# Order of the expert groups in the dense stage of a hybrid decoder block: stored first products spread among the others

## The chip, the core and the metric

The kernel runs on one core of one Trainium2 chip. The metric is the device time of one execution in microseconds (us), lower is better. PE is TensorE, DVE is VectorE, ACT is ScalarE, POOL is GpSimd, and SP is the engine whose queue starts most of the DMA transfers. A number such as L1254 is a line of the kernel before.

## What is computed

The reference is one layer of a decoder for 1024 tokens of width 1024: two attention branches, a memory attention, and a mixer with 16,384 experts of which each token uses 128. The last part is the one in question:

```python
def chunk(args):
    hc, ic, gc = args
    a = jnp.einsum('cd,ced->ce', hc, u[ic])
    a = jax.nn.gelu(a, approximate=False) * gc.astype(hc.dtype)
    return jnp.einsum('ce,ced->cd', a, v[ic])
```

`ic` holds the 128 chosen experts of each token and `gc` their weights. The sum over the experts may be taken in any order.

## The kernel before

The tokens are handled in eight blocks of 128. For blocks 0 to 3 the chosen rows of `u` and `v` are gathered from DRAM, one row per token at a time. POOL starts each gather (L1035 for `u`, L1051 for `v`) into a ring of seven tiles `rows`, and DVE multiplies and sums the gathered tile (L1038 for `u`, L1057 for `v`). This is a side stream: a pacer (`Pace`) hands out one gather for every so many estimated microseconds of PE work, 2.0 in the dense stage (`U_EACH[-1]`).

For blocks 4 to 7, 512 tokens together, all experts are computed densely, in 128 tiles of 128 experts (`dense`, L1192). Per tile there is a first product (`first`, L1210: 24 matmuls with the tile `uT`, after `uraw` was loaded and split on ACT and DVE into two parts), a gelu, a multiplication with the expert weights `wl` (L1254, on DVE; a weight is zero where the token did not choose the expert), a split of the result into the two parts `c0` and `c1` (ACT L112, DVE L113), and a second product with the rows of `v` (L1278, after `vraw` was loaded and split, 24 matmuls per tile). Tiles go in groups of four: `group` (L1241) makes the four operands `c`, `second` (L1260) does 96 matmuls with them. The loop asks for `group` of the next group before `second` of the present one. Four of the eight accumulators stay in PSUM (`kept`); the other four (`out`) are added to SBUF by DVE after each group (`accu`, L1283).

The first 48 tiles (`EARLY`) have their first product done in an earlier stage, in which the weights are made. Their gelu is stored to DRAM (`ga`), and in the dense stage `group` only loads it back (L1250) instead of computing it. I call the twelve groups of these tiles early groups, and the other twenty full groups.

Three buffers matter. The reloaded gelu has one buffer (`c`, L1249), so the load for the next early tile starts only after the multiplication of the one before. `wl` has two buffers, each for two tiles (L1245), so a new one can be loaded only when both tiles of the pair before last are split. And the operands `c0`, `c1` have seven buffers (L1255) where two groups would need eight, so the last split of a group waits for the end of the second product before it.

All engines take their instructions in the order in which they were built. That order comes from the order of the code and from priorities that lag the gathers; nothing is reordered when it runs.

Of the kernel before, what the change touches and what calls it, by code (L numbers as in the profile page):

```python
# [84 lines left out]
class K:  # L85
# [1106 lines left out]
    def dense(self, psum, early):  # L1192

        nc, a = self.nc, self.a
        blks = list(range(NG, NB))
        V = a["peer_v"][0]
        NE = P
        with ExitStack() as ctx:
            E = ctx.enter_context
            up = E(self.pool("up"))  # L1200
            h3 = self.h3T

            def load_u(e):
                raw = up.tile([P, D], F32, name="uraw", bufs=U_BUFS)
                self.last_load = nc.sync.dma_start(raw, a["peer_ut"][e]).ins
                uT = [up.tile([P, KD, P], F32R, name=f"uT{j}", bufs=2) for j in range(2)]
                self.split(raw.rearrange("p (k c) -> p k c", k=KD), uT[0], uT[1])
                return uT

            def first(e):  # L1210
                uT = load_u(e)
                o = self.acc()
                for k in range(KD):
                    self.mm3(o, [u[:, k] for u in uT], [x[:, k] for x in h3], k == 0, k == KD - 1)
                self.pace.tick(KD * 3 * 0.216)
                return o

            ga = {}
            with ExitStack() as c2:
                self.wb = c2.enter_context(self.pool("wb"))  # L1220
                self.u_each = U_EACH[-2]
                self.pace.add("weights", self.weights(blks))
                for e in range(early):
                    o = first(e)
                    t = self.wb.tile([P, 512], F32, name="gelu", bufs=2)
                    nc.scalar.activation(t, o, AF.Gelu)
                    ga[e] = self.scratch([P, 512], f"ga{e}")
                    nc.sync.dma_start(ga[e], t)
                self.pace.drain("weights")
            self.route_ctx.close()  # L1230
            psum = self.psum_phase(psum, "ps3", A_BUFS)
            kept = {}
            for n in range(KEEP):
                i, d = n % ND, n // ND
                kept[i, d] = self.ps.tile([P, 512], F32, name=f"kept{n}", bufs=1)
            self.u_each = U_EACH[-1]
            sp = E(self.pool("sp"))
            accu = sp.tile([P, ND, D], F32, name="accu")
            G = 4

            def group(gi):  # L1241
                cs = []
                for e in range(gi * G, gi * G + G):
                    if e % 2 == 0:
                        w2 = sp.tile([P, 2 * ND, 2, P // 2], F32, name="wl", bufs=2)  # L1245
                        nc.sync.dma_start(w2, self.Wd[:, :, e:e + 2].rearrange("j p e n -> p j e n"))
                    w = w2[:, :, e % 2]
                    if e in ga:
                        c = sp.tile([P, DT], F32, name="c", bufs=1)  # L1249
                        nc.sync.dma_start(c, ga[e])  # L1250
                    else:
                        c = first(e)
                        nc.scalar.activation(c, c, AF.Gelu)
                    nc.vector.tensor_tensor(w, c.rearrange("p (j n) -> p j n", j=2 * ND), w, op=OP.mult)  # L1254
                    ch = [sp.tile([P, DT], F32R, name=f"c{j}", bufs=7) for j in range(2)]  # L1255
                    self.split(w, *[x.rearrange("p (j n) -> p j n", j=2 * ND) for x in ch])
                    cs.append(ch)
                return cs

            def second(gi, cs):  # L1260
                vs = []
                for e in range(gi * G, gi * G + G):
                    vv = [sp.tile([P, D], F32R, name=f"v{j}", bufs=V_BUFS[j]) for j in range(2)]
                    raw = sp.tile([P, D], F32, name="vraw", bufs=V_BUFS[2])
                    nc.sync.dma_start(raw, V[e * P:(e + 1) * P])
                    self.split(raw, vv[0], vv[1])
                    vs.append(vv)
                for i in range(ND):
                    for d in range(2):
                        ds = slice(d * 512, (d + 1) * 512)  # L1270
                        keep = (i, d) in kept
                        o = kept[i, d] if keep else self.ps.tile([P, 512], F32, name="out", bufs=O_BUFS)
                        last = gi == NE // G - 1
                        for j in range(G):
                            self.mm3(o, [c[:, i * P:(i + 1) * P] for c in cs[j]], [v[:, ds] for v in vs[j]],
                                     j == 0 and (gi == 0 or not keep), j == G - 1 and (last or not keep))
                        if keep:
                            if last:  # L1278
                                nc.scalar.activation(accu[:, i, ds], o, AF.Copy)
                        elif gi == 0:  # L1280
                            nc.scalar.activation(accu[:, i, ds], o, AF.Copy)
                        else:
                            nc.vector.tensor_tensor(accu[:, i, ds], accu[:, i, ds], o, op=OP.add)  # L1283
                        self.pace.tick(G * 3 * 0.216)

            cs = group(0)
            for gi in range(NE // G):
                nx = group(gi + 1) if gi + 1 < NE // G else None
                second(gi, cs)
                cs = nx  # L1290
            for i, b in enumerate(blks):
                t = [up.tile([P, D], F32, name="uraw", bufs=U_BUFS) for _ in range(2)]
                self.finish(b, accu[:, i], t if i else t + [sp.tile([P, D], F32, name="vraw", bufs=V_BUFS[2])])
        return psum
# [136 lines left out]
```

## Time and profile before

| | us |
|---|---|
| median of three runs | 3481.64 |
| lowest and highest run | 3471.62 and 3495.5 |
| the profiled execution | 3480.88 |
| span of its trace | 3479.1 |

The profiled execution is as long as the median run to within 0.02%. Its span starts with the first instruction; 1.8 us lie outside. The dense stage starts at about 2200 us; the early groups run to about 2540 and the full groups from there to the end. Waits in a trace are given as the idle time of an engine before an instruction and the event that ended it.

### The profile page before, as it was taken

To read this page: it belongs to the slowest core of one execution; us is meant where nothing else is said; L and a number is where in the kernel's file an instruction comes from. 1 tells how busy PE (TensorE), PEld (TensorE's weight loads), DVE (VectorE), ACT (ScalarE), POOL (GpSimd) and SP (SyncE) were. 2 spreads that over 40 slices of the span, in tenths; PEclk is the share of its full clock that TensorE was granted. 3 is DMA by queue.
4 is the path that set the end of the run, shared out by engine and by line. 5 is a ranking of instruction groups with operands and counts; after the bars stand their busy time and mean duration, and the time that the engine had idled before them with its cause. 6 is when DMAs were issued, how large, how long until landed. Compare 5 with 4: busy or idle time off the path is not lost. (4 is left out here: it accounts for less than half of the span.)

```text
span 3479.1 us, 42293 instructions
## 1 busy us (share of the span) xinstructions
PE 3023.2 (87%) x13234; PEld 2293.0 (66%) x13234; DVE 2849.2 (82%) x6623; ACT 1404.7 (40%) x2537; POOL 1396.1 (40%) x1122
## 2 busy tenths in 40 slices
PE   8999888798788798777899897588899999999997
PEld 6778765553345675545777675466677887877886
DVE  6656544588969889888999899677799999999998
ACT  5756344345656451322455557222122222222222
POOL 0010000011245346554123566334456666676664
PEclk9999998899888799778999999799899999999999
DMA  4575444435699479888567999999999999999997
GB/s 139 164 183 139 164 140 138 134 121 182 197 299 317 139 246 366 308 319 299 167 222 272 381 384 389 360 303 309 312 348 375 379 378 357 368 384 379 382 376 269
DMA packets 394209, 964.64 MB, mean 277 GB/s; under 512 B 36712, under 2 KB 146048, under 8 KB 392576
## 3 DMA queue, kind: packets, MB, share of 16 engines
q0 software_dynamic: 155264, 560.01, 45.4%
q1 hardware_dynamic: 238720, 401.94, 33.7%
q8 instruction: 104, 1.70, 0.2%
q14 instruction: 121, 0.99, 0.1%
HBM read 871.64 MB, written 90.18 MB: 276 GB/s over the span
## 5 line engine op out<-in xcount | busy, mean ns | idle before, releaser
L1035 POOL DMA_INDIRECT rows<-in_peer_u_dram,ii x512 | 679.8, 1328 | 903.9 <-DVE rows L1038 284.2
L1051 POOL DMA_INDIRECT rows<-in_peer_v_dram,ii x512 | 652.9, 1275 | 419.8 <-DVE h3s L1057 269.0
L1057 DVE SCALAR_TENSOR_TENSOR h3s<-rows,wexp,h3s 128x1024 f32<-128x1024 f32 x508 | 650.8, 1281 | 34.9 <-DMA rows<-in_peer_v_dram,ii 26.0
L1038 DVE SCALAR_TENSOR_TENSOR rows<-rows,h3s 128x1024 f32<-128x1024 f32 x512 | 610.2, 1218 | 72.5 <-DMA rows<-in_peer_u_dram,ii 72.1
L135 PE MATMUL acc<-fT,uT 128*128 128x512 f32 x1024 | 417.0, 407 | 39.1 <-ACT uT L112 21.7
L137 PE MATMUL acc<-fT,uT 128*128 128x512 f32 x1024 | 410.1, 400 | 3.1 <-DVE uT L113 3.0
L136 PE MATMUL acc<-fT,uT 128*128 128x512 f32 x1024 | 409.8, 400 | 0.0
L112 ACT ACTIVATE c<-wl 128x512 fp32r<-128x512 f32 x128 | 80.0, 631 | 758.9 <-PE out L136 458.9
L149 POOL TENSOR_TENSOR rstd<-msq,mhalf 128x1 f32<-128x1 f32 (+1 forms) x42 | 34.4, 819 | 595.1 <-DVE msq L147 578.3
L135 PEld LDWEIGHTS acc<-fT,uT 128*128 128x128 f32 x1024 | 195.9, 191 | 85.2 <-ACT uT L112 22.1
L136 PE MATMUL kept<-v,c 128*128 128x512 f32 x512 | 206.1, 406 | 38.0 <-DVE v L113 37.9
L135 PE MATMUL kept<-v,c 128*128 128x512 f32 x512 | 201.7, 400 | 38.1 <-ACT v L112 38.1
L137 PEld LDWEIGHTS acc<-fT,uT 128*128 128x128 f32 x1024 | 195.4, 191 | 59.3 <-issue 12.3
L112 ACT ACTIVATE uT<-uraw 128x1024 fp32r<-128x1024 f32 x128 | 135.6, 1059 | 235.8 <-PE acc L136 162.0
L136 PEld LDWEIGHTS acc<-fT,uT 128*128 128x128 f32 x1024 | 195.9, 191 | 39.6 <-issue 0.7
L135 PE MATMUL out<-v,c 128*128 128x512 f32 x512 | 203.9, 398 | 9.3 <-DVE accu L1283 9.3
L113 DVE TENSOR_TENSOR w<-wraw,w 128x512 fp32r<-128x512 f32 (+1 forms) x176 | 116.4, 679 | 116.2 <-ACT w L112 109.2
L137 PE MATMUL kept<-v,c 128*128 128x512 f32 x512 | 204.3, 399 | 0.0
L136 PE MATMUL out<-v,c 128*128 128x512 f32 x512 | 203.5, 397 | 0.0
L137 PE MATMUL out<-v,c 128*128 128x512 f32 x512 | 203.3, 397 | 0.0
L568 ACT ACTIVATE junk<-W,xb 128x384 bf16<-128x384 f32 (+5 forms) x186 | 163.7, 880 | 78.4 <-DVE xb L566 75.6
L133 PE MATMUL acc<-wraw,hT 128*128 128x512 f32 (+1 forms) x384 | 168.7, 593 | 15.7 <-ACT tok L355 10.0
(361 smaller groups left out, 6710.7 us busy)
## 6 DMA issues: line engine op xcount, KB each, us to landing
uraw<-in_peer_ut_dram SPq DMA_DIRECT2D x128, 512.0 KB, 8.6
vraw<-in_peer_v_dram SPq DMA_DIRECT2D x128, 512.0 KB, 8.7
Wd<-wbuf SPq DMA_DIRECT2D x64, 512.0 KB, 9.1
wl<-Wd SPq DMA_DIRECT2D x64, 512.0 KB, 9.6
wraw<-in_w_in_dram SPq DMA_DIRECT2D x40, 512.0 KB, 3.7
fraw<-in_w_in_dram SPq DMA_DIRECT2D x32, 512.0 KB, 5.8
wraw<-in_w_out_dram SPq DMA_DIRECT2D x24, 512.0 KB, 3.7
ga<-gelu SPq DMA_DIRECT2D x48, 256.0 KB, 5.3
```

Of the source, the lines that this page charges most:

```text
L112: self.nc.scalar.activation(hi, src, AF.Copy)
L113: self.last_dve = self.nc.vector.tensor_tensor(lo, src, hi.bitcast(F32), op=OP.subtract).ins
L133: self.last_pe = nc.tensor.matmul(out, l[0], r[0], start=start, stop=stop).ins
L135: nc.tensor.matmul(out, l[0], r[0], start=start, stop=False)
L136: nc.tensor.matmul(out, l[0], r[1], start=False, stop=False)
L137: self.last_pe = nc.tensor.matmul(out, l[1], r[0], start=False, stop=stop).ins
L149: nc.gpsimd.tensor_tensor(r, v, self.mhalf[:, :n], op=OP.pow)
L568: nc.scalar.activation(junk[:, :(b + 1) * P], self.W[b], AF.Sign, bias=xb[:, j:j + 1].bitcast(F32), accum_out=s[:, j:j + 1])
L1035: nc.gpsimd.indirect_dma_start(out=u, out_offset=None, in_=a["peer_u"][0], in_offset=bass.IndirectOffsetOnAxis(ap=ii[:, j:j + 1], axis=0))
L1038: nc.vector.scalar_tensor_tensor(u, u, 1.0, h3, op0=OP.mult, op1=OP.mult, accum_out=aa[:, j:j + 1])
L1051: nc.gpsimd.indirect_dma_start(out=v, out_offset=None, in_=a["peer_v"][0], in_offset=bass.IndirectOffsetOnAxis(ap=r["ii"][:, j:j + 1], axi ...
L1057: nc.vector.scalar_tensor_tensor(o, v, w[:, j:j + 1], o, op0=OP.mult, op1=OP.add)
```

## The change

The order of the 32 groups in the dense stage is no longer 0, 1, ..., 31, with the twelve early groups in front. A list `order` puts an early group at every second or third place: positions 2, 5, 7, 10, 13, 15, 18, 21, 23, 26, 29 and 31 (counted from 0). The first two groups are full ones, and the last is an early one. Nothing else changes: the same transfers, the same matmuls, the same buffers.

```diff
@@ in dense(), between group() and second() @@
+            n, m = NE // G, early // G
+            early_ones, others = iter(range(m)), iter(range(m, n))
+            order = [next(early_ones if (k + 1) * m // n > k * m // n else others) for k in range(n)]
...
-                        last = gi == NE // G - 1
+                        last = gi == order[-1]
                         for j in range(G):
                             self.mm3(o, [c[:, i * P:(i + 1) * P] for c in cs[j]], [v[:, ds] for v in vs[j]],
-                                     j == 0 and (gi == 0 or not keep), j == G - 1 and (last or not keep))
+                                     j == 0 and (gi == order[0] or not keep), j == G - 1 and (last or not keep))
...
-                        elif gi == 0:
+                        elif gi == order[0]:
...
-            cs = group(0)
-            for gi in range(NE // G):
-                nx = group(gi + 1) if gi + 1 < NE // G else None
+            cs = group(order[0])
+            for k, gi in enumerate(order):
+                nx = group(order[k + 1]) if k + 1 < n else None
                 second(gi, cs)
                 cs = nx
```

What this does to the instruction order is shown on DVE and on SP. The first place is on DVE, where the first two multiplications of an early group stand. The names: `wl<-c` is the multiplication with a reloaded gelu, `wl<-acc` the one after a first product, `c1<-wl` the split of its result, `rows,aa<-rows,h3s` a gathered row of `u`, `uT1<-uraw` and `v1<-vraw` the splits of loaded weights, `accu<-accu,out` the addition of a second product. Before, in the middle of an early group, between two second products:

```order
L1254 TENSOR_TENSOR wl_20303<-c_20312,wl_20303 128x8x64
L1038 SCALAR_TENSOR_TENSOR rows_20091,aa_19500<-rows_20091,h3s_19498 128x1024
L1283 TENSOR_TENSOR accu_18901<-accu_18901,out_20358 128x512
L1038 SCALAR_TENSOR_TENSOR rows_20094,aa_19500<-rows_20094,h3s_19498 128x1024
L1038 SCALAR_TENSOR_TENSOR rows_20165,aa_19500<-rows_20165,h3s_19498 128x1024
L1283 TENSOR_TENSOR accu_18901<-accu_18901,out_20393 128x512
L1254 TENSOR_TENSOR wl_20477<-c_20479,wl_20477 128x8x64
L1038 SCALAR_TENSOR_TENSOR rows_20182,aa_19500<-rows_20182,h3s_19498 128x1024
L1038 SCALAR_TENSOR_TENSOR rows_20197,aa_19500<-rows_20197,h3s_19498 128x1024
L1038 SCALAR_TENSOR_TENSOR rows_20217,aa_19500<-rows_20217,h3s_19498 128x1024
L1283 TENSOR_TENSOR accu_18901<-accu_18901,out_20425 128x512
L1254 TENSOR_TENSOR wl_20477<-c_20486,wl_20477 128x8x64
```

In the changed kernel the same two multiplications (of `wl_20317`) stand inside the first products of a full group:

```order
L113 TENSOR_TENSOR c1_20065<-wl_19977,c0_20064 128x512
L1038 SCALAR_TENSOR_TENSOR rows_19954,aa_19420<-rows_19954,h3s_19418 128x1024
L1038 SCALAR_TENSOR_TENSOR rows_19974,aa_19420<-rows_19974,h3s_19418 128x1024
L113 TENSOR_TENSOR uT1_20515<-uraw_20512,uT0_20514 128x1024
L1254 TENSOR_TENSOR wl_20068<-acc_20076,wl_20068 128x8x64
L1038 SCALAR_TENSOR_TENSOR rows_19971,aa_19420<-rows_19971,h3s_19418 128x1024
L113 TENSOR_TENSOR c1_20110<-wl_20068,c0_20109 128x512
L1254 TENSOR_TENSOR wl_20317<-c_20319,wl_20317 128x8x64
L1038 SCALAR_TENSOR_TENSOR rows_20013,aa_19420<-rows_20013,h3s_19418 128x1024
L1038 SCALAR_TENSOR_TENSOR rows_20010,aa_19420<-rows_20010,h3s_19418 128x1024
L1254 TENSOR_TENSOR wl_20068<-acc_20119,wl_20068 128x8x64
L1254 TENSOR_TENSOR wl_20317<-c_20326,wl_20317 128x8x64
```

The load of `wl_20317` needs the buffer of `wl_19977`, which the first of these rows gives free; seven rows later the load is wanted. Before, `wl_20477` needs the buffer of `wl_20287`, free 10 us of DVE work earlier. The second place is on DVE as well, where one second product follows directly on another. Before:

```order
L113 TENSOR_TENSOR c1_20126<-wl_20113,c0_20125 128x512
L113 TENSOR_TENSOR v1_20320<-vraw_20321,v0_20319 128x1024
L1283 TENSOR_TENSOR accu_18901<-accu_18901,out_20270 128x512
L113 TENSOR_TENSOR c1_20293<-wl_20287,c0_20292 128x512
L113 TENSOR_TENSOR c1_20300<-wl_20287,c0_20299 128x512
L113 TENSOR_TENSOR v1_20326<-vraw_20327,v0_20325 128x1024
L1254 TENSOR_TENSOR wl_20303<-c_20305,wl_20303 128x8x64
L113 TENSOR_TENSOR v1_20332<-vraw_20333,v0_20331 128x1024
L113 TENSOR_TENSOR c1_20309<-wl_20303,c0_20308 128x512
L113 TENSOR_TENSOR v1_20338<-vraw_20339,v0_20337 128x1024
L1254 TENSOR_TENSOR wl_20303<-c_20312,wl_20303 128x8x64
```

And in the changed kernel:

```order
L113 TENSOR_TENSOR c1_20156<-wl_20068,c0_20155 128x512
L113 TENSOR_TENSOR c1_20323<-wl_20317,c0_20322 128x512
L1288 TENSOR_TENSOR accu_18901<-accu_18901,out_20300 128x512
L113 TENSOR_TENSOR c1_20330<-wl_20317,c0_20329 128x512
L113 TENSOR_TENSOR v1_20350<-vraw_20351,v0_20349 128x1024
L113 TENSOR_TENSOR v1_20356<-vraw_20357,v0_20355 128x1024
L1254 TENSOR_TENSOR wl_20333<-c_20335,wl_20333 128x8x64
L113 TENSOR_TENSOR v1_20362<-vraw_20363,v0_20361 128x1024
L113 TENSOR_TENSOR c1_20339<-wl_20333,c0_20338 128x512
L113 TENSOR_TENSOR v1_20368<-vraw_20369,v0_20367 128x1024
L1038 SCALAR_TENSOR_TENSOR rows_20262,aa_19420<-rows_20262,h3s_19418 128x1024
L1254 TENSOR_TENSOR wl_20333<-c_20342,wl_20333 128x8x64
```

The two have the same kinds of rows from the first `c1` to the second `wl<-c`, in almost the same order: the buffer that the first `c1` gives free is loaded for the `wl` that is multiplied after two more `c1`, an `accu` and two `v1`. The third place is the queue of SP around these loads. Before:

```order
L1250 DMA c_20296<-ga33_16822 128x512
L1250 DMA c_20305<-ga34_16939 128x512
L1246 DMA wl_20303<-Wd_13635 128x8x128
L1265 DMA vraw_20511<-in_peer_v_dram 128x1024
L1246 DMA wl_20477<-Wd_13635 128x8x128
L1250 DMA c_20312<-ga35_17049 128x512
L1265 DMA vraw_20517<-in_peer_v_dram 128x1024
L1265 DMA vraw_20523<-in_peer_v_dram 128x1024
L1250 DMA c_20479<-ga36_17179 128x512
L1265 DMA vraw_20529<-in_peer_v_dram 128x1024
L1250 DMA c_20486<-ga37_17252 128x512
```

And in the changed kernel:

```order
L1205 DMA uraw_20603<-in_peer_ut_dram 128x1024
L1246 DMA wl_20317<-Wd_13635 128x8x128
L1205 DMA uraw_20646<-in_peer_ut_dram 128x1024
L1250 DMA c_20326<-ga5_14113 128x512
L1250 DMA c_20335<-ga6_14166 128x512
L1205 DMA uraw_21045<-in_peer_ut_dram 128x1024
L1246 DMA wl_20333<-Wd_13635 128x8x128
L1246 DMA wl_20510<-Wd_13635 128x8x128
L1270 DMA vraw_20694<-in_peer_v_dram 128x1024
L1250 DMA c_20342<-ga7_14271 128x512
```

The loads of `uraw` for the next first products now stand between and behind the reloads of `c`.

## Rows read from the trace of the kernel before

**Rows 1.** Windows of the dense stage: early groups, full groups, a quiet piece, the end.
```profile
core 0: us, PE busy (x) PEld busy (x) DVE busy (x) ACT busy (x) POOL busy (x), PEclk, DMA share, GB/s
2221.00:2540.00 319.00, 264.72 (x1029) 208.78 (x1030) 247.19 (x342) 73.70 (x97) 120.40 (x93) 0.89 0.91 309
2540.00:3400.00 860.00, 840.90 (x3651) 690.02 (x3651) 818.06 (x998) 238.84 (x309) 573.04 (x421) 0.99 1.00 374
2700.00:2900.00 200.00, 200.00 (x882) 165.25 (x881) 197.02 (x190) 55.27 (x71) 130.30 (x100) 1.00 1.01 378
3400.00:3479.10 79.10, 60.60 (x266) 49.50 (x265) 66.27 (x68) 18.74 (x28) 34.70 (x27) 0.90 0.74 262
```

**Rows 2.** Waits of DVE from 2221 us on: total, times, longest.
```profile
DVE wl L1254 <- DMA c<-ga: 44.1, 25, 10.0
DVE rows L1038 <- DMA rows<-in_peer_u_dram,ii: 34.9, 26, 4.6
DVE wl L1254 <- DMA wl<-Wd: 21.4, 5, 6.8
...
DVE wl L1254 <- issue: 5.1, 2, 3.1
```

**Rows 3.** Waits of PE from 2221 us on.
```profile
PE kept L135 <- ACT v L112: 38.1, 2, 35.3
PE kept L136 <- DVE v L113: 37.9, 17, 4.8
PE acc L135 <- DVE wl L1254: 17.5, 9, 3.7
```

**Rows 4.** Timeline of DVE where an early group follows another: start, duration, instruction, [idle before].
```profile
2373.11 1.22 DVE L1038 SCALAR_TENSOR_TENSOR rows<-rows,h3s 128x1024 f32<-128x1024 f32 x1
...
2374.26 0.69 DVE L113 TENSOR_TENSOR c<-wl,c 128x512 fp32r<-128x512 f32 x1
2374.87 1.22 DVE L113 TENSOR_TENSOR v<-vraw,v 128x1024 fp32r<-128x1024 f32 x1
2376.00 0.68 DVE L1283 TENSOR_TENSOR accu<-accu,out 128x512 f32<-128x512 f32 x1
2376.60 1.28 DVE L113 TENSOR_TENSOR c<-wl,c 128x512 fp32r<-128x512 f32 x2
2377.80 1.22 DVE L113 TENSOR_TENSOR v<-vraw,v 128x1024 fp32r<-128x1024 f32 x1
2382.55 0.69 DVE L1254 TENSOR_TENSOR wl<-c,wl 128x512 f32<-128x512 f32 x1 [3.53 <-DMA wl<-Wd]
2383.16 1.22 DVE L113 TENSOR_TENSOR v<-vraw,v 128x1024 fp32r<-128x1024 f32 x1
...
2387.54 0.69 DVE L1254 TENSOR_TENSOR wl<-c,wl 128x512 f32<-128x512 f32 x1 [1.43 <-DMA c<-ga]
```

**Rows 5.** Timeline of SP's DMA queue at the same place.
```profile
2374.97 0.37 SPq L1246 DMA_DIRECT2D wl<-Wd  x1
...
2383.27 0.32 SPq L1250 DMA_DIRECT2D c<-ga  x1
```

**Rows 6.** DMA issues from 2230 to 2530 us: count, KB each, median us to landing.
```profile
vraw<-in_peer_v_dram SPq DMA_DIRECT2D x42, 512.0 KB, 5.6
c<-ga SPq DMA_DIRECT2D x45, 256.0 KB, 4.6
wl<-Wd SPq DMA_DIRECT2D x22, 512.0 KB, 7.4
```

**Rows 7.** DMA issues from 2560 to 2900 us, in the full groups.
```profile
vraw<-in_peer_v_dram SPq DMA_DIRECT2D x31, 512.0 KB, 10.1
...
wl<-Wd SPq DMA_DIRECT2D x15, 512.0 KB, 10.0
```

**Rows 8.** Timeline of DVE at the start of the dense stage.
```profile
2209.71 1.28 DVE L1057 SCALAR_TENSOR_TENSOR h3s<-rows,wexp,h3s 128x1024 f32<-128x1024 f32 x1 [0.34 <-DMA rows<-in_peer_v_dram,ii]
2220.99 0.69 DVE L1254 TENSOR_TENSOR wl<-c,wl 128x512 f32<-128x512 f32 x1 [10.00 <-DMA c<-ga]
```

## The prediction

> **What bounds the kernel now.** I read the windows of the dense stage first. The full groups, from 2540 us on, run close to every limit at once: PE is busy 841 of 860 us, DVE 818, and the DMA share is 1.00. In the early groups, 2221 to 2540, DVE is busy only 247 of 319 us, PE 265 at a granted clock of 0.89, and the DMA share is 0.91 [rows 1]. This is the loose part, and the reader is to ask which wait makes it so.
>
> The waits answer that. From 2221 us on DVE waits 44.1 us for reloaded gelus `c`, 21.4 us for weights `wl`, 5.1 us in two waits for which the profile names no releaser, at the same kind of instruction (I count them with `wl`), and 34.9 us for gathered rows of `u` [rows 2]. The first three, 70.6 us, lie in the early groups. With DVE's busy time they fill the 319 us: 247 + 71 = 318. So DVE works or waits for a transfer there, and never waits long for PE. PE's waits are for DVE (the split of `v`, 37.9 us) or at the start [rows 3]. The chain in the early groups is therefore DVE, and what stretches it are transfers that land too late. In the quiet piece of the full groups, 2700 to 2900, nothing is loose: PE takes 200/882 = 0.227 us per matmul without a gap and DVE is busy 197 us [rows 1].
>
> **The change part by part.** The amount of work stays. DVE's is 247 + 818 + 66 = 1132 us from 2221 to the end [rows 1]. PE's in the groups is 12 x 96 + 20 x 192 = 4992 matmuls, at 0.227 us 1133 us. Early and full groups also have DVE and PE work in nearly the same proportion, a full group twice an early one of each, so mixing them evens out no load between these two engines. What mixing can change is the waits of DVE. So I price those, place by place, for the twelve early groups.
>
> How late a load is follows from its round trip less the DVE work between release and use. DVE's steps, from one start to the next, are 0.6 us for a `c1`, `wl` or `accu` row, 1.13 for a split of `v` or `uraw`, and 1.15 for a gathered row [rows 4]. For `wl` before, where two second products meet, a split of `v`, an `accu`, two `c1` and another split of `v` stand between the `c1` that gives the buffer free and the use: 4.1 us, from 2374.87 to 2378.9 [rows 4]. There were seven such waits, 21.4 + 5.1 = 26.5 us, 3.8 each [rows 2]; one of them is 3.53 us [rows 4], where SP starts the load at 2374.97 and the use begins at 2382.55 [rows 5]. The round trip of `wl` in the early groups is thus 4.1 + 3.8 = 7.9 us. For `c`, started at 2383.27 and used at 2387.54, it is about 4.3 us, of which 2.9 are covered and 1.43 waited for [rows 4, 5].
>
> In the changed kernel each early group has four multiplications with reloaded gelus, and the order gives these gaps:
> - The first, inside the first products of a full group, needs a `wl` whose buffer comes free only 5.9 us of DVE work before (4.7 in four of the twelve groups; on average 5.5). Before, the same load had 10 to 12 us. Wait: 7.9 - 5.5 = 2.4 us.
> - The second follows 2.9 us after the first, and the single buffer `c` has to be reloaded between them. Before, this gap was 7 to 9 us. Wait: 1.4 us.
> - The third stands where two second products meet, with the same 4.1 us as before. Wait: 3.8 us.
> - The fourth has 2.9 to 5.2 us for its `c`. Wait: 1.0 us, a little less than the 1.43.
>
> Together 8.6 us per early group, 12 x 8.6 = 103 us. That is the lower end, for it uses round trips of the early groups. In the full groups transfers take longer: a load of `vraw` 10.1 us to landing instead of 5.6, one of `wl` 10.0 instead of 7.4 [rows 6, 7]. If the early groups, now placed among full ones, meet those times, the two `wl` waits grow by 2.6 us each. For `c` no row in the full groups exists; by the ratio of `vraw`, 1.8, its 4.6 us become 8.3, and the two `c` waits grow by 3.7 us each. That makes 21.2 us per group and 254 us in all, the upper end.
>
> Which end is nearer? The DMA engines have a fixed amount to move: 0.91 x 319 + 1.00 x 860 = 1150 us of full business in 1179 us [rows 1]. If the stage gets 50 to 60 us longer, the share is 1150 in some 1234, 0.93 everywhere. This lies about a fifth of the way from the 0.91 of the early groups to 1.00. I take that: 103 + 0.2 x 151 = 133 us.
>
> Against this stand two credits. The 34.9 us of waits for gathered rows of `u` lie almost all in the full groups [rows 2]; while DVE waits for a `wl` or a `c`, the ring of seven row tiles fills, so some of these waits go. I take 15 us, between 0 and 35. And the start: before, DVE waits 10.0 us for the first `c` [rows 8], and PE 35.3 us for the first `v` [rows 3]. Now the first group is a full one, and PE can do first products meanwhile. But the accumulators of two tiles are all that it may fill before DVE has a `wl`, whose load stands in the same queue as before. I take 5 of the 10 us, between 0 and 10; PE's head start of two tiles, 48 matmuls or 11 us, is worth nothing while DVE is the chain.
>
> The queue of SP is blocked while a reload of `c` waits for its buffer, and now loads of `uraw` stand behind it. I cost this at nothing: the `uraw` behind the blocked reload is wanted only after the following second product, some 20 us later. Without that cover each blocked stretch of about 5 us would fall on PE.
>
> **The sum.** New early waits 133, less the old 70.6, less 15 for the rows, with the start's 5 that remain: 133 + 5 - 71 - 15 = +52 us. From the profiled execution, 3480.9, which stands within 0.02% of the median 3481.64, this gives 3533 us, 1.5% slower.
>
> **The rivals.**
>
> *The waits go away, faster.* Mixing relieves the DMA engines around the early groups, loads land in time, and the 70.6 us vanish: 3481 - 71 = 3410 us. The place is the four multiplications of each early group; it decides for this rival if a `c` comes round in under 2.9 us and a `wl` in under 4.1 us. For it speaks that the early groups are the loose part, with PE at a clock of 0.89 [rows 1]. Against it: the DMA share there is the lowest of the stage, and still `c` took 4.6 and `wl` 7.4 us to landing [rows 6]; in the company of full groups they will not get quicker. The Trainium skill, "DMA: Bandwidth & Descriptors", section on the anatomy of one DMA, gives a fit of about 2.0 us plus the bytes at 436 GB/s, for a transfer on its own (measured there for those that POOL starts). As an estimate from that page 256 KB take 2.6 us and 512 KB 3.2 us, both inside the gaps, so by that rule this rival would be the outcome and no wait would remain. The trace disagrees: with 4.6 and 7.4 us the transfers queue behind others, and I go by the trace.
>
> *No change.* The early waits rise only to the lower end, 103 us, and the row waits in the full groups (35 us) are swallowed whole: 103 + 5 - 71 - 35 = +2, or 3483 us. For it: the row waits are of the same kind, DVE running ahead of DMA, and every pause of DVE lets rows arrive. Against it: the waits for rows fall in half of the full groups only, the new waits in all of them.
>
> *Much slower.* DMA stays at a share of 1.00 around the early groups, and the full groups' landing times hold: 254 + 5 - 71 - 15 = +173, or 3654 us. Against it: in so long a stage the share would be 1150/1350 = 0.85, under that of the early groups, so these times can't persist.
>
> **How the numbers follow.** The forecast gets a chance of 0.46, no change 0.34, faster 0.12, much slower 0.08. A measurement of this kernel can tell about 1%, 35 us, from no change. Faster by more than that is the first rival, 0.12; within it is the second, 0.34; slower is the forecast and the last, 0.54. The range goes from 3465 us, a little below the second rival, for credits larger than I took, to 3595 us, where the waits lie halfway between their ends (103 + 76 + 5 - 71 = +113). It leaves out most of the first and of the third rival.
>
> **What would show it.** Right: in the changed trace DVE waits for `wl` about 24 times, twice per early group, 3 to 5 us each, and about as often for `c`, 1 to 2 us each; the sum of both is well over 71 us; the loose windows are gone, and instead every stretch with an early group has PE busy some 90%. The waits for rows of `u` are below 35 us. Wrong: DVE's waits for `wl` and `c` below 60 us in all, or PE waiting long in first products for `uraw`, or a DMA share that rises to 1.00 in every window while the stage gets shorter. If the waits are there and the time is not longer, DVE was not the chain, and PE's idle time must have fallen instead.

## Result, and the profile after

The changed kernel takes 3584.53 us (3578.94 to 3591.68, four runs); the kernel before, on the same chip, 3487.05 us. The ratio is 1.0286, with a 95% interval of 1.0241 to 1.033. It is slower by 97 us, where 52 were forecast. The profiled execution's span is 3577.2 us against 3479.1: 98.1 us longer.

The windows of the stage, cut as in [rows 1]; the last ends with the span.
```profile
core 0: us, PE busy (x) PEld busy (x) DVE busy (x) ACT busy (x) POOL busy (x), PEclk, DMA share, GB/s
2221.00:2540.00 319.00, 284.17 (x1180) 229.10 (x1179) 263.68 (x365) 85.59 (x112) 172.90 (x126) 0.95 0.92 329
2540.00:3400.00 860.00, 774.51 (x3220) 623.94 (x3219) 719.78 (x889) 208.54 (x272) 465.73 (x347) 0.94 0.93 332
2700.00:2900.00 200.00, 183.47 (x758) 147.47 (x757) 169.61 (x170) 47.07 (x62) 103.05 (x79) 0.93 0.92 325
3400.00:3577.20 177.20, 131.37 (x543) 105.15 (x542) 149.45 (x150) 35.34 (x49) 89.06 (x69) 0.89 0.84 286
```
The loose stretch at the start has become a little tighter (PE 284 us instead of 265), and the 860 us that were tight are loose now: DVE 720 us instead of 818, PE 775 instead of 841. DVE's work in the three windows is the same, 1132.9 us against 1131.5. So nothing was added to DVE but waiting, and what has to be asked is for what it waits. (PE's matmuls from 2200 us on take 1192.0 us instead of 1166.2, at a mean granted clock of 0.93 instead of 0.95; but DVE's waits for PE, at `accu`, grow only from 7.0 to 8.8 us, so the lower clock is not seen to lengthen the chain.) DVE's waits from 2200 us on (2200, not 2221, so that the wait at the start counts; before, the totals of [rows 2] are the same from 2200):
```profile
DVE wl L1254 <- DMA wl<-Wd: 142.4, 22, 10.6
DVE rows L1038 <- DMA rows<-in_peer_u_dram,ii: 28.2, 25, 3.6
DVE wl L1254 <- DMA c<-ga: 14.4, 7, 4.0
DVE wl L1254 <- issue: 11.6, 3, 4.0
```
Weights, gelus and the waits without a named releaser come to 168.4 us against 70.6, +97.8, about the whole loss (its other waits together change by -2.5). It is the kind of wait that moved: `c`, 44.1 us before, has almost gone, and `wl` went from 21.4 to 142.4. PE's waits from 2200 us on, which answer to [rows 3], are all for DVE, and they are consequences (L1288 is L1283 of the kernel before):
```profile
PE kept L136 <- DVE v L113: 61.3, 19, 6.3
PE out L135 <- DVE accu L1288: 56.1, 22, 5.6
PE acc L135 <- DVE wl L1254: 45.3, 7, 29.1
```

The first multiplication of an early group, in the middle of a full group's first products, on DVE and on SP's queue:
```profile
2373.05 0.68 DVE L113 TENSOR_TENSOR c<-wl,c 128x512 fp32r<-128x512 f32 x1
...
2378.82 0.68 DVE L113 TENSOR_TENSOR c<-wl,c 128x512 fp32r<-128x512 f32 x1
2388.39 0.69 DVE L1254 TENSOR_TENSOR wl<-c,wl 128x512 f32<-128x512 f32 x1 [8.89 <-DMA wl<-Wd]
...
2391.92 0.69 DVE L1254 TENSOR_TENSOR wl<-c,wl 128x512 f32<-128x512 f32 x1
```
```profile
2367.42 6.10 SPq L1205 DMA_DIRECT2D uraw<-in_peer_ut_dram  x2
2373.76 0.38 SPq L1246 DMA_DIRECT2D wl<-Wd  x1
2377.19 0.33 SPq L1205 DMA_DIRECT2D uraw<-in_peer_ut_dram  x1
```
The split at 2373.05 gives the buffer free, SP asks at 2373.76, DVE has 5.8 us of work until 2379.5, and the weights are used at 2388.39: 14.6 us from issue to use. The second multiplication, at 2391.92, does not wait at all: its `c` came round in under 3 us, asked for at 2389.11. In the window from 2355 to 2392 us the DMA share is 0.7 or more up to 2386 us and 0.1 to 0.6 behind it, so that this reload met DMA engines that had largely drained. The third, where a full group's second products end (answers to [rows 4, 5]):
```profile
2413.51 0.72 DVE L113 TENSOR_TENSOR c<-wl,c 128x512 fp32r<-128x512 f32 x1
2414.15 2.35 DVE L113 TENSOR_TENSOR v<-vraw,v 128x1024 fp32r<-128x1024 f32 x2
2420.82 0.69 DVE L1254 TENSOR_TENSOR wl<-c,wl 128x512 f32<-128x512 f32 x1 [4.33 <-DMA wl<-Wd]
...
2426.84 0.69 DVE L1254 TENSOR_TENSOR wl<-c,wl 128x512 f32<-128x512 f32 x1 [1.31 <-DMA c<-ga]
```
Taken over all twelve early groups, from these two timelines:

| multiplication | forecast wait, low to high end | measured, mean of 12 | issue to use, mean (least to most) |
|---|---|---|---|
| first (`wl`, inside a full group) | 2.4 to 5.0 | 7.1 (sum 85.2) | 12.7 (7.4 to 15.4) |
| second (`c`) | 1.4 to 5.1 | 0.1 (sum 1.3) | |
| third (`wl`, between second products) | 3.8 to 6.4 | 4.9 (sum 58.2) | 8.9 (7.3 to 12.1) |
| fourth (`c`) | 1.0 to 4.7 | 1.1 (sum 13.1) | |

With 10.6 us at the start these make the 168.4. The third and fourth lie near the forecast; the first is above its upper bound. The gaps came out as worked out: issue to use less wait is 5.6 us for the first (forecast 5.5) and 4.0 for the third (4.1).

### The profile page after: what moved, and what is told of

The parts are those of the page before. It is cut to its first block, busy times and chain, and to the rows that moved or that the text cites. A ratio compares the mean times of both kernels' runs of the same rounds, so it can differ in the third digit from the quotient of the medians.

```text
span 3577.2 us, 42240 instructions
## 1 busy us (share of the span) xinstructions
PE 3049.6 (85%) x13234; PEld 2306.6 (64%) x13234; DVE 2853.5 (80%) x6623; ACT 1405.0 (39%) x2537; POOL 1391.8 (39%) x1122
## 5 line engine op out<-in xcount | busy, mean ns | idle before, releaser
L136 PE MATMUL kept<-v,c 128*128 128x512 f32 x512 | 209.5, 410 | 61.3 <-DVE v L113 61.3
L135 PE MATMUL out<-v,c 128*128 128x512 f32 x512 | 210.7, 412 | 56.1 <-DVE accu L1288 56.1
L137 PE MATMUL kept<-v,c 128*128 128x512 f32 x512 | 206.3, 403 | 0.0
L136 PE MATMUL out<-v,c 128*128 128x512 f32 x512 | 205.7, 402 | 0.0
L137 PE MATMUL out<-v,c 128*128 128x512 f32 x512 | 205.3, 401 | 0.0
L135 PE MATMUL kept<-v,c 128*128 128x512 f32 x512 | 203.5, 406 | 0.0
```

Source lines behind the costliest of these rows:

```text
L135: nc.tensor.matmul(out, l[0], r[0], start=start, stop=False)
L136: nc.tensor.matmul(out, l[0], r[1], start=False, stop=False)
L137: self.last_pe = nc.tensor.matmul(out, l[1], r[0], start=False, stop=stop).ins
```

## Experiments

**Theory**: an early pair inherits a buffer of `wl` that a full group's middle still holds, so its load is asked for some 5 us ahead of a use that it reaches after 9 to 13. **Rivals**: the reload of `c` blocks SP's queue; SP's queue itself is the long way; the DMA engines are full, so that an earlier load delays something else. The kernel before took 3481.7 to 3488.8 us beside them. All eighteen, with DVE's waits from 2200 us on, in us, summed from that view ("weights, gelus": `wl`, `we`, `c` and unnamed at L1254; "all": every wait of DVE):

| kernel | time | ratio, 95% interval | span | weights, gelus | rows | all |
|---|---|---|---|---|---|---|
| before | | | 3479.1 | 70.6 | 44.2 | 133 |
| after | 3584.5 | 1.0286, 1.0241 to 1.0330 | 3577.2 | 168.4 | 33.2 | 228 |
| a_runs4 | 3520.2 | 1.0106, 1.0076 to 1.0136 | 3519.5 | 97.9 | 46.7 | 167 |
| a_last | 3539.0 | 1.0141, 1.0104 to 1.0177 | 3535.2 | 69.5 | 75.0 | 183 |
| a_wl3 | 3539.8 | 1.0156, 1.0124 to 1.0187 | 3541.2 | 108.7 | 43.4 | 190 |
| a_c2 | 3583.2 | 1.0278, 1.0256 to 1.0300 | 3586.5 | 159.1 | 42.1 | 233 |
| a_we2wl1 | 3593.0 | 1.0308, 1.0285 to 1.0331 | 3588.0 | 204.7 | 22.6 | 245 |
| a_we_v3 | 3597.6 | 1.0298, 1.0262 to 1.0335 | 3601.7 | 87.0 | 27.9 | 253 |
| a_v3 | 3649.6 | 1.0466, 1.0428 to 1.0505 | 3648.5 | 139.0 | 26.1 | 294 |
| a_we_r6 | 3569.9 | 1.0239, 1.0206 to 1.0272 | 3571.4 | 116.6 | 62.7 | 197 |
| a_r6 | 3609.7 | 1.0357, 1.0328 to 1.0386 | 3609.3 | 158.8 | 58.5 | 245 |
| a_wlact | 3622.7 | 1.0407, 1.0362 to 1.0451 | 3617.3 | 207.0 | 25.4 | 268 |
| a_wl3act | 3579.0 | 1.0271, 1.0225 to 1.0318 | 3575.1 | 153.8 | 38.6 | 227 |
| a_runs4wl3 | 3503.6 | 1.0059, 1.0033 to 1.0085 | 3492.4 | 95.6 | 36.3 | 148 |
| b_wl3 | 3482.2 | 0.9989, 0.9973 to 1.0004 | 3475.5 | 77.1 | 35.3 | 133 |
| b_c2 | 3485.5 | 1.0002, 0.9984 to 1.0020 | 3469.0 | 71.2 | 29.9 | 123 |
| b_wlact | 3484.4 | 1.0003, 0.9981 to 1.0024 | 3474.1 | 81.9 | 30.2 | 128 |
| b_wl3c2ch6 | 3483.4 | 0.9988, 0.9969 to 1.0006 | 3482.8 | 64.6 | 38.9 | 132 |
| b_wl3c2r6 | 3538.8 | 1.0158, 1.0130 to 1.0185 | 3536.8 | 66.4 | 70.7 | 172 |
| b_wl3c2v3 | 3587.8 | 1.0278, 1.0245 to 1.0311 | 3598.8 | 30.6 | 28.3 | 244 |

a_ kernels have the mixed order (but for a_runs4, a_runs4wl3 and a_last, which have orders of their own), b_ kernels the order of before. Read the spans and the last column together: against before, the span's growth and that of DVE's waits agree within some 8 us in every run, but for the three with a buffer of rows less, where 18 to 29 us of the span are in no listed wait. In those three the stage before ends 19 to 31 us later (its last matmul for the weights, `dot`, is at 2194.7 to 2206.6 us instead of 2176.0), so that 16 to 28 us more of DVE's work fall behind 2200 us. The agreement by itself follows from DVE's work being the same and would hold for any engine. That DVE is the chain in the changed kernel is read from who ends the waits: PE's are ended by DVE, and most of DVE's by transfers (194 of 228 us).

### Is it the step from a full group to an early one?

a_runs4, then a_last:
```diff
-            order = [next(early_ones if (k + 1) * m // n > k * m // n else others) for k in range(n)]
+            order = [next(early_ones if k % 11 in (2, 3, 4, 5) and k < 32 else others) for k in range(n)]
```


> The early groups spread in three runs of four instead of one by one. Only the first group of each run has the tight gap (4.6 to 5.9 us) at its first multiplication, the other nine have 10 to 12 us. Theory: nine of the twelve waits of 7.1 us go, 64 us, and some 10 us of waits for c come back as in the order of before: 3585 - 64 + 10 = 3531 us, between 3515 and 3548. Rival, that any early group in the company of full ones waits because transfers are slower there: little change, 3570 to 3590 us.


```diff
-            order = [next(early_ones if (k + 1) * m // n > k * m // n else others) for k in range(n)]
+            order = list(range(m, n)) + list(range(m))
```


> All full groups first, the twelve early groups after them back to back, so that an early group follows a full one once, not eleven times. Theory (the price is that of each step from a full group to an early one): one wait of 5 to 10 us at that step, then the waits of the early stretch as in the kernel before (some 70 us), 3475 to 3510 us. Rival (early groups are dear wherever they stand behind full ones, or the end of the program can't hide them): 3550 us or more.

With three steps in place of twelve the time was 3520 us, as the theory had it. The waits of DVE in a_runs4:
```profile
DVE wl L1254 <- DMA wl<-Wd: 65.6, 13, 11.0
DVE rows L1038 <- DMA rows<-in_peer_u_dram,ii: 40.7, 30, 4.6
DVE wl L1254 <- DMA c<-ga: 20.5, 11, 3.9
```
First multiplications inside a full group, with 9 to 13 us from issue to use, stood only at the heads of the three runs. With one step (a_last) weights and gelus cost what they cost before, 69.5 us, but the time was 3539, not 3475 to 3510: that is a miss. What the theory had left out were the rows:
```profile
DVE rows L1038 <- DMA rows<-in_peer_u_dram,ii: 64.0, 31, 8.3
...
DVE h3s L1057 <- DMA rows<-in_peer_v_dram,ii: 11.0, 11, 2.3
```
Waits for rows are 75.0 us against 44.2. No matmul runs after 3500 us, and DVE still adds up rows until 3527. So the early groups are a poor end of the stage, for another reason than the one tested.

### Is it the buffer?

a_wl3 (the room comes from three small tiles, `rz`, `zg`, `aa`, each held to two buffers; the same shrink stands in every kernel below with `we` or `wl3` in its name, not in the others):
```diff
-                        w2 = sp.tile([P, 2 * ND, 2, P // 2], F32, name="wl", bufs=2)
+                        w2 = sp.tile([P, 2 * ND, 2, P // 2], F32, name="wl", bufs=3)
```


> The changed order with a third buffer for wl (and one buffer less for aa, two less for two small tiles, to make room). Theory: DVE is the chain, and a wait is the round trip of a wl load less the DVE work between the release of its buffer and its use. In the built order the third buffer is not turned into more work between the two: the multiplications move ahead, and the gaps stay at 4.7 to 8.7 us (5.9 on average for the first pair of a group, 5.2 for the second), all inside first products, where the round trip was 13 us. So the waits for wl stay at 140 to 180 us and the time at 3570 to 3625 us. Rival, that two buffers are too few: the third takes the waits away, 3585 - 140 = 3445 us.

a_c2:
```diff
-                        c = sp.tile([P, DT], F32, name="c", bufs=1)
+                        c = sp.tile([P, DT], F32, name="c", bufs=2)
```


> The changed order with two buffers for the reloaded gelu c. Theory: only the 14 us of waits for c can go, the waits for wl (154 us) stay, for their gaps are the same: 3570 us, between 3560 and 3585. Rival, that the reloads of c hold up SP's queue and the wl loads behind them: waits for wl fall by half or more, 3500 us or less.

A second `c` changes nothing (3583 us), so the reload of `c` does not hold the mixed order back, and does not block it through SP's queue. A third `wl` gives back 45 us: more than the theory of its expectation (nothing) and less than its rival (140), so both missed. The waits of a_wl3 say why:
```profile
DVE wl L1254 <- DMA wl<-Wd: 57.1, 17, 11.4
DVE wl L1254 <- DMA c<-ga: 45.3, 21, 7.0
```
Of the 85 us that `wl` lost, `c` took over 31, rows and `accu` some 24 more. Then own buffers (`we`) for the early groups: two beside one `wl`, and two beside two, where the room was taken from `vraw` or from the ring of rows, each with a control that takes only the room:
```diff
-                        w2 = sp.tile([P, 2 * ND, 2, P // 2], F32, name="wl", bufs=2)
+                        w2 = sp.tile([P, 2 * ND, 2, P // 2], F32, name="we" if e in ga else "wl", bufs=2)
...
-U_BUFS, V_BUFS = 3, (4, 4, 4)
+U_BUFS, V_BUFS = 3, (4, 4, 3)
```
(a_we_v3; a_v3 has the second half alone, without the three small tiles of which its expectation speaks. a_we_r6 has in its place `R_BUFS` 6 for 7, as a_r6 alone. a_we2wl1 has `bufs=2 if e in ga else 1`, and neither.)

> The changed order, with two wl buffers of their own (named we) for the early groups, so that an early group's weights no longer queue for a buffer that a full group's middle still holds; one vraw buffer fewer makes room. Theory (the loss is the weights asked for too late, about 5.5 us ahead of a use that they reach after 12.7 us): VectorE's waits for wl and we together fall from 142.4 us to under 40 us, no wait of 9 us stands at an early group's first pair, and the time is 3445 to 3500 us. Rival (the DMA engines are full, so a transfer asked for earlier only delays rows and c, and the waits change their name): waits for c and rows rise by over 50 us and the time is 3520 to 3590 us.

> Control for the run before: the changed order with one vraw buffer fewer and the same small buffers shrunk, wl left as it is. If these shrinks cost nothing, the time is that of the changed kernel, 3570 to 3600 us, with 130 to 155 us of VectorE waits for wl. If fewer rows in flight also let the weights land sooner, the waits for wl fall under 110 us and the time is 3540 to 3570 us; if the rows are short of a buffer, waits for rows rise over 60 us and the time is over 3600 us.

> The changed order, two buffers of their own for the early groups (we) beside two wl, one buffer of rows fewer in place of the one vraw of the earlier run. Theory: the waits for wl and we fall under 40 us, the waits for rows rise by less than 40 us, 3460 to 3520 us. Rival (own buffers can't bring it below the third shared buffer, because c and PE take the waits over): 3530 us or more.

> Control: the changed order with six buffers of rows, not seven, and no other edit of the weights. If one buffer of rows costs nothing, 3575 to 3600 us with 130 to 155 us of waits for wl. If fewer gathers in flight let the weights land sooner (the 12.7 us of a load in a full group's middle are the DMA engines' queue), the waits for wl fall under 120 us; if the rows then come late, their waits rise from 28 us to over 50 us.

> The changed order, with two weight buffers (we) for the early groups alone and one (wl) for the full groups: as many bytes as the third wl buffer of the earlier run, nothing taken from rows or vraw. Theory (the price is the buffer that an early pair inherits from the full group's middle): VectorE's waits for wl and we fall from 142.4 us to under 45 us and the time is 3470 to 3520 us, below the 3540 us of three shared buffers. Rival (one buffer is too few for the full groups, or an earlier load only moves the wait to c and PE): 3530 to 3590 us.

None came below a_wl3, and every forecast of a large gain was a miss. Against their controls own buffers gave 52 us (3598 and 3650) and 40 us (3570 and 3610; a_we_r6 came to the stage another 12 us later than its control), about what the third shared buffer gave. The control for `vraw` (one buffer less of it, and nothing else) was dear by itself, 65 us over the changed kernel. Its waits show for what:
```profile
DVE wl L1254 <- DMA wl<-Wd: 113.9, 22, 10.0
DVE v L113 <- ACT v L112: 64.9, 16, 7.3
```
One buffer of rows less cost 25 us. Much of that is not a price of this stage, for the stage before ended 19 us later in this profile; from 2200 us on the waits for rows rose (58.5 against 33.2) and others fell. The waits for `wl` stayed at 138 us, so a shorter ring of rows did not let the weights land sooner. In a_we_r6 the waits were for `we` 47.0, for `c` 48.8 us: once weights come sooner, `c` is late. a_we2wl1 shows the other side: with one buffer the full groups wait themselves, 76.3 us for `wl`.

The buffer is thus part of the price, about 45 us of 97. More buffers were not tried without taking room from what also binds; three `wl` with two `c` in the mixed order stays open for that reason.

### SP's queue, or the engines that all queues share?

a_wlact; b_wlact is the same edit in the order of before, a_wl3act adds the third buffer:
```diff
-                        nc.sync.dma_start(w2, self.Wd[:, :, e:e + 2].rearrange("j p e n -> p j e n"))
+                        (nc.scalar if e in ga else nc.sync).dma_start(w2, self.Wd[:, :, e:e + 2].rearrange("j p e n -> p j e n"))
```


> The changed order; the early groups' weights are asked for on ScalarE's queue, right behind the split that frees their buffer, in place of SP's. Own-queue theory (the load stands behind two uraw loads on SP's queue): the first pair's time from issue to use falls from 12.7 us to 7 to 9 us, VectorE's waits for wl from 142.4 us to 70 to 100 us, and the time to 3510 to 3550 us. Shared-engines theory (the sixteen DMA engines are full in a full group's products, whichever queue asks): issue to use stays at 11 to 14 us, waits at 125 to 155 us, 3570 to 3600 us.

> The order of before with the early groups' weights on ScalarE's queue. There the load meets few uraw loads, so both theories expect little: waits for wl from 26.5 us to 15 to 30 us, and 3475 to 3492 us. Under 3465 us would show that SP's queue held the early stretch back too.

> The third wl buffer and ScalarE's queue together. If queue and buffer are two parts of the price, waits for wl fall below the 57.1 us of the third buffer alone, to 15 to 40 us, and the time from 3540 to 3500 to 3525 us; if the engines are the limit, 3530 to 3550 us as with the buffer alone.

The own-queue theory falls, and further than its rival had it: 3623 us, 38 more than the changed kernel, and a_wl3act 39 more than a_wl3 (42 and 40 by the ratios). Neither branch of these two expectations held; b_wlact came out as expected. DMA issues of a_wlact (2230 to 3530 us), and below of b_wlact (2230 to 2530, its early groups); count, KB, median us to landing:
```profile
wl<-Wd SPq DMA_DIRECT2D x37, 512.0 KB, 9.3
wl<-Wd ACTq DMA_DIRECT2D x23, 512.0 KB, 13.1
```
```profile
wl<-Wd ACTq DMA_DIRECT2D x21, 512.0 KB, 5.5
```
The two lines for ScalarE's queue settle the main question. The load, the queue, the buffers and the early group's own work are the same in both; what differs is the order, and with it the neighbours. The same load takes 5.5 us among early groups and 13.1 among full ones. That is what the prediction had put at "a fifth of the way".

Why ScalarE's queue lost time shows when the twelve early groups are taken place by place. At the first multiplication the load took 12.5 us from issue to use, as on SP's queue (12.7). At the third it took 12.6 instead of 8.9, and DVE's waits there grew from 58 to 98 us; at the first they grew from 85 to 96. At the third place two loads of weights are asked for together, the early group's and the next full group's. The DMA queues in the changed kernel from 2412.4 to 2420.9 us, from the load's issue to its use, and below in a_wlact, from 2411.8 to 2425.6:
```profile
q1 hardware_dynamic: 1297, 0.66, 26.9%
```
```profile
q1 hardware_dynamic: 1057, 0.74, 17.4%
q10 hardware_dynamic: 1040, 0.52, 14.4%
```
A load of weights has 1040 packets. On SP's queue (q1) 257 packets of other loads passed with it; with a queue of its own (q10), 1057 packets of SP's queue passed meanwhile. So in this group, the only one counted, the load had another neighbour, which on SP's queue had stood behind it.

At the first place the main neighbour is the gathers: in the kernel before their queue moved 12672 packets from 2230 to 2530 us, 42 per us, and 24326 from 2560 to 2900, 72 per us. What that does can be counted in one such load of a_wlact. The DMA queues from 2372 to 2388 us: packets, MB, share of sixteen engines; then the load, asked for at 2372.69:
```profile
q0 software_dynamic: 912, 3.29, 52.2%
q1 hardware_dynamic: 384, 1.36, 21.5%
q10 hardware_dynamic: 1040, 0.52, 11.4%
...
wl<-Wd ACTq DMA_DIRECT2D x1, 512.0 KB, 14.3
```
q10 is ScalarE's and holds this load alone: 1040 packets of half a KB, 65 on each engine. q0 holds the gathers, in packets of 3.6 KB; 57 of them, nearly one for each packet of the load, ran on each engine meanwhile, and 24 of SP's. By the shares a packet takes 0.147 us on q0, 0.143 on q1 and 0.028 on q10 (share x 16 us x 16 engines / packets), so an engine needed 65 x 0.028 + 57 x 0.147 + 24 x 0.143 = 13.6 us for all. (That is the busy share of the 16 us, 85%, taken apart; the load itself took 14.3.) The load's own part is 1.8 us. In the other eleven first loads of a_wlact the gathers' packets were 408 to 943, never more than the load's own 1040; the three loads with under 700 landed in 7.2 to 10.2 us, the other nine in 12.3 to 14.8. (A slower load also sees more packets pass, and no run changed the gathers alone, so this is a count and not yet a cause.) The Trainium skill, "DMA: Bandwidth & Descriptors", section on queues, rings and completion order, says that an engine goes round the queues that have work and takes a whole packet of each, typically of 9 to 17 descriptors. The counts here, nearly one packet of the gathers for each of the load's, go with such turns; whether the trace's packets are those of that page it does not show. That packets of half a KB are what makes this load so easy to delay was worked out, not tried: no run changed how `Wd` is laid out.

### Was there something to win without mixing?

b_wl3, b_c2 and b_wl3c2ch6 relieve the early stretch of before, each in another place (edits as above; b_wl3c2ch6 takes the room from the split halves):
```diff
-                    ch = [sp.tile([P, DT], F32R, name=f"c{j}", bufs=7) for j in range(2)]
+                    ch = [sp.tile([P, DT], F32R, name=f"c{j}", bufs=6) for j in range(2)]
```


> The order of before with the same third buffer for wl. Here the gap between release and use grows to 12 to 20 us in most places (7 to 8 in five). Theory: the 26.5 us of waits for wl go nearly all, 3487 - 25 = 3462 us, between 3450 and 3472. Rival, that the early groups are bound by the bytes that the DMA engines move: the waits come back as waits for c or rows, and the time stays at 3480 to 3492 us.

> The order of before with a second c buffer and nothing else. If c's single buffer is what binds the early stretch, waits for c fall from 44.1 us to under 15 us, those for wl rise from 26.5 us by less than 25 us, and the time is 3455 to 3478 us. If wl takes over at once (it is reloaded through two buffers), the waits only change their name: wl 50 to 75 us, 3478 to 3495 us.

> The order of before with three wl buffers and two c buffers, room made by one pair of split halves (c0, c1) fewer; rows and vraw keep theirs. Theory (the early stretch was bound by its two single reloads): waits for wl and c from 2200 us on fall from 70.6 us to under 35 us, 3440 to 3475 us. Rival (the missing half delays the next group's multiplications, or the transfers bind): 3480 to 3530 us.

All three end at no change. Waits of DVE in b_wl3, and below in b_c2, against 44.1 for `c` and 21.4 for `wl` in [rows 2]:
```profile
DVE wl L1254 <- DMA c<-ga: 63.5, 23, 10.1
...
DVE wl L1254 <- DMA wl<-Wd: 4.1, 2, 2.5
```
```profile
DVE wl L1254 <- DMA wl<-Wd: 33.5, 9, 6.4
DVE wl L1254 <- DMA c<-ga: 28.2, 10, 10.1
```
The named waits do go, and their sum stays: 77.1, 71.2 and 64.6 us against 70.6. The two with room from `vraw` or rows were worse:

> The order of before, with a third wl buffer and a second c buffer. Theory (in the early stretch each of the two buffers alone ends the wait when the other has been relieved, so both have to be): waits for wl and c from 2200 us on fall from 70.6 us to under 30 us and the time is 3425 to 3460 us. Rival (the stretch is bound by the transfers themselves, so the waits move to rows or PE): 3470 to 3490 us, as with the third wl buffer alone (3482).

> The order of before, with a third wl buffer and a second c buffer, room made by one buffer of rows (with a vraw buffer fewer it took 3588 us). Theory (c and wl were the early stretch's only waits, and vraw was what spoilt the earlier run): their waits from 2200 us on fall from 70.6 us to under 30 us, 3430 to 3465 us. Rival (the stretch is bound by the transfers, waits move to rows and v): 3475 us or more.

b_wl3c2v3 more than halves the waits for weights and gelus to 30.6 us, but DVE waits 123.2 us for ACT at the splits of `v`; b_wl3c2r6 waits 70.7 us for rows, and its stage starts 21 us later. Both point to the room that was taken; a control for it was not run in this order. Last, the two edits that gave back most, joined (three runs of four, third `wl`):

> Three runs of four early groups (three steps from full to early) with the third wl buffer. If the price is per step and per inherited buffer, both gains add in part: waits for wl fall from 65.6 us to 20 to 40 us, c takes some over, and the time is 3485 to 3510 us. If mixing as such can win once the waits go (the rival of the prediction that ended faster), under 3470 us. If c takes all over, 3515 us or more.

It came to 3503.6 us as forecast, 0.6% over before; its waits for `wl`, 43.2 us, are just over their forecast. The gains add in part, and the best mixed order found is still not below the order of before. No version tried beats both kernels.

## Why the prediction was right in kind and short in size

- **DVE as the chain** was right: its work is unchanged, PE's waits are ended by DVE, and of the 98 us all but a few are DVE's waits for weights and gelus. One reading of the prediction was loose: in 247 + 71 = 318 the 71 hold the 10.0 us at the start, which lie ahead of 2221 us. Within the window 60.6 us are weights and gelus, and small waits for rows and `accu` make up the rest.
- **Where the waits would be** was right for `wl`: 25 waits, the three unnamed and the one at the start among them, where 24 were forecast. For `c` it was wrong: seven waits, not 24. After a long wait for weights the next `c` came round in under 3 us (2391.92 above), not in the 4.3 that was assumed, on DMA engines that had largely drained at that place; the other places were not looked at for that.
- **The step that failed** is the term for the new waits, "a fifth of the way" between the ends, 133 us. The share came out as worked out, 0.93 in the 860 us window, but landing does not follow the mean share: the load at the first multiplication took 12.7 us to its use, more than the 10.5 of the upper end (7.9 + 2.6), the one at the seam 8.9, near the lower end of 7.9. First multiplications cost 85 us where 2.4 x 12 = 29 was the low end and 60 the high one; `c` gave some back (14 us where 29 was the low end). In all the new waits were 158 us, 25 over the term. That the miss is no larger is partly luck: by the fifth the four places were to cost 35, 26, 52 and 21 us and cost 85, 1, 58 and 13, so that 57 us were priced too low and 32 too high, and the second hid more than half of the first. a_wlact against b_wlact shows that the neighbours set the landing; a_runs4, with three steps in place of twelve, lost 70 us of these waits.
- **The two credits** were each too large. Waits for rows of `u` fell by 6.7 us, not 15. The start gave nothing: 10.6 us for the first `wl` instead of 10.0 for the first `c`, where half had been taken off. With 158 + 10.6 - 70.6 - 6.7 = 91 us, 7 of the 98 are left for small things, such as 4.0 us of a wait for `uraw` at the very end (L1070). The whole miss of 46 us is 25 for the new waits, 8 for the rows, 6 for the start and these 7.
- **SP's queue blocked by `c`**, costed at nothing: right by a_c2.
- **The rivals.** "The waits go away" and "no change" fall with the wait view. "Much slower" rested on full groups' landing everywhere; it was right for the first multiplication alone, and the argument against it, that the mean share would sink, did not protect that one.

## What to carry to other kernels

Price a moved load by the landing time at the place where it will be issued, position by position, and not by a mean share of the DMA engines: the same load took 5.5 us beside one neighbour and 13.1 beside another. A ring of two buffers that is ample for one kind of tile can be the bottleneck for the tile that follows it; runs of like tiles pay that price once per run. Where a chain waits for several reloads in turn, relieving one renames the wait: add up all waits of the chain before believing a gain, and run a control for the buffer that the edit took its room from.

## What was not expected of the hardware

- A second hardware queue gained nothing at one place and lost time at another: from issue to use 12.5 us against 12.7 on SP's queue at the first multiplication, 12.6 against 8.9 at the third. (The medians of 13.1 and 9.3 us above compare different places: those on SP's queue are mostly loads of full groups.) The Trainium skill, "DMA: Bandwidth & Descriptors", section "Issuing engines are not separate DMA queues", says that transfers started by different engines run on the same sixteen DMA engines and interleave; the trace agrees, with 1057 packets of SP's queue beside the 1040 of the load on ScalarE's.
- A load of 512 KB that goes in 1040 packets took 14.3 us, in which gathers with packets seven times as large ran nearly one for one with it; its own packets were 1.8 us of that.
- One buffer of `vraw` less cost 65 us and one of rows 25 us (much of it ahead of the stage) in the mixed order, against the 40 to 52 us that buffers for the weights gave back.
